# A two-block transformer forward pass on one core: later modulation, another router front end, expert sums on GpSimd, another order

## The chip, the cores and the metric

The kernel runs on 1 core of a Trainium2 chip. The metric is the time of one execution in device microseconds (us). A core has five engines that run their own instruction queues: TensorE (PE, matrix products and transposes), VectorE (DVE), ScalarE (ACT), GpSimd (POOL) and SyncE (SP, which here only issues transfers). Sixteen DMA engines move data between HBM and the on-chip memory (SBUF). Results of PE land in PSUM banks, from which DVE or ACT take them. An engine executes its queue in order: a waiting instruction holds everything behind it.

## The reference, cut to what matters

256 tokens of width 1024, all in fp32. Block 1 is one layer: retention and sliding-window attention side by side, then a mixture of experts (top 1 of 4 groups, top 2 of its 8 experts), then a gate fed by a second input `p`. Block 2 is two layers on the result `x` and on a context stream `ctx`, each layer with three branches and a feed-forward part, shifted and scaled by a modulation vector.

```python
# block 1
z = rms_norm(x, mix_norm_g) @ w_in
x = x + (sigmoid(gate_r) * retention(...) + sigmoid(gate_s) * attention(q, k, v)) @ w_out
h = rms_norm(x, ffn_norm_g)
g_prob = softmax(h @ w_rg + b_rg)               # 4 groups: the best one
e_logits = h @ w_re + b_re                      # its 8 experts: the best two
x = x + sum_over_two(weight * expert(h))        # SwiGLU, 1024 -> 256 -> 1024
x = x + sigmoid(rms_norm(x, ple_gate_norm_g) @ w_ple_gate) * rms_norm(p @ w_ple, ple_norm_g)
# block 2, twice
mod = silu(c) @ w_mod[l] + b_mod[l]             # 6 vectors of 1024; a second row for ctx
h = rms_norm_2(x, g_norm1) * (1 + sc1) + sh1
x = x + gt1 * (merge of 3 branches of h @ w_in[l]) @ w_out[l]
x = x + gt2 * relu(modulated norm(x) @ w1)**2 @ w2
```

The context stream goes through layer 0 in full; layer 1 takes only its keys and values.

## The kernel before, in words

Every dense weight arrives in pieces of 128x1024 fp32 (512 KB). SP loads a piece into `raw` (8 buffers, line L229), ACT rounds it into a high part `wh` (L187), DVE subtracts that from it to get the low part `wl` (L188), and PE makes three products for each (high·high, high·low, low·high): lines L245 to L247 where the weight is the stationary operand (`dense_a`), L268 to L270 where it moves (`dense_b`). So each piece costs a transfer, one ACT and one DVE pass, and 24 or 12 matmuls.

The program is one thread of Python that emits instructions; a tile scheduler then orders each engine's queue from dependences and priorities. Side jobs are generators put `beside` the main one: `advance()` moves each forward by a share of a step for each dense piece, `drain` runs the rest. Side jobs are: the modulation product `w_mod` of layer 0 during block 1 and that of layer 1 later (each step loads two pieces of `w_mod` at L704 and lets PE do four narrow matmuls with `sT` at L709), and the experts during the context's layer.

The stages: block 1's projections, first q, k, v of the windowed attention (L268 to L270 into `pd`), then its heads (transposes L533, L539, scores L551), retention, `w_out`. Then `router`: it loads its tables on the GpSimd queue (L736 to L746), sums squares of the rows of `xres` on ACT (L291), takes 1/rms by Newton steps on DVE (L178 to L183), scales the rows on DVE (L760), stores them to `xnscr` in HBM (L762), transposes them on PE (L767), multiplies by the router's weights (L772), and by a long chain of small steps forms the list of slots (PE L869, DVE L872). GpSimd gathers the rows of the first group of four experts into `m_he` (L913), PE transposes these (L925) and runs the experts: up and gate L935, down L954; weights lie in 8 buffers `ew`. Each group's result goes to `oscr` in HBM (L961). After the last group, GpSimd gathers each token's two results back into `m_ob` (L965, two buffers) and DVE adds weight times result to `xres` (L967). Then `moe_overflow` reads a count on every engine (L973) and branches over a rarely needed path (L974), and `ple_turn` normalizes `xres` (ACT L291, L322; DVE L321) and transposes it (L332) for the gate. The context stream's feed-forward part runs beside all that; its result `xc` is stored by GpSimd (L1654). After that come the two layers of x.

Of the kernel before, what the change touches and what calls it, by code (L numbers as in the profile page):

```python
# [9 lines left out]
F32 = mybir.dt.float32  # L10
# [10 lines left out]
D = 1024  # L21
T = 256
# [141 lines left out]
class Build:  # L164
    def __init__(self, nc, tc, ins, out, dbg=None):
# [5 lines left out]
        self.sturn = 0  # L171

# [66 lines left out]
    def mm_a(self, ps, x, w, f):  # L239
# [4 lines left out]
        for k, (wh, wl) in enumerate(w):  # L244
            mm(ps, wh[:, s], xh[:, k], start=k == 0, stop=False)  # L245
            mm(ps, wh[:, s], xl[:, k], start=False, stop=False)  # L246
            mm(ps, wl[:, s], xh[:, k], start=False, stop=k == n - 1)  # L247
# [9 lines left out]
    def dense_b(self, st, x, view, put, width=512):  # L257
# [3 lines left out]
        for c in range(0, view.shape[2], width):  # L261
            ps = [st.dense()[:, :width] for _ in range(2)]
            for k0, w in self.pieces(st, view[:, :, c:c + width]):
                for t in range(2):
                    s = slice(t * 128, t * 128 + 128)
                    for j, (wh, wl) in enumerate(w):
# [3 lines left out]
                        mm(ps[t], xl[:, k, s], wh, start=False, stop=k == K - 1)  # L270
# [86 lines left out]
    def run_all(self):  # L357
        nc, tc, i = self.nc, self.tc, self.i
        with ExitStack() as ctx:
# [114 lines left out]
    def block1_mix(self, st):  # L474
# [34 lines left out]
        self.dense_b(st, xT, w[:, :, 2560:2816], put_kv, width=256)  # L509
        gq8 = one.tile([128, 1], F32, name="gq8")  # L510
# [6 lines left out]
        nc.sync.dma_start(decay, i["decay"])  # L517
        rq = self.newton(st, ssq, 16, 1.0 / 64)
# [24 lines left out]
        for t in range(2):  # L543
# [32 lines left out]
            for hp in range(4):  # L576
# [8 lines left out]
                self.split(ysT[0][:, hp, ts], ysT[1][:, hp, ts], ps)  # L585

# [7 lines left out]
        STs = [held()[:, :768].rearrange("p (h s) -> p h s", h=2) for _ in range(2)]  # L594
# [99 lines left out]

    def w_mod(self, st, tag, l):
        nc, i = self.nc, self.i
        mm = nc.tensor.matmul
        for j in range(3):
            ps = self.psum.tile([128, 512], F32, name=tag, tag=tag, bufs=2)
            for k in range(8):  # L700
# [4 lines left out]
                with self.tc.high_priority(offset=CLUSTER):  # L705
                    for u in (1, 0):
                        for v in range(2):
                            g = 2 * u + v
                            mm(ps[32 * g:32 * g + 32], self.sT[:, k], wt[u][:, v * 512:v * 512 + 512], start=k == 0,  # L709
                               stop=False, tile_position=(0, 32 * g))  # L710
                yield
            brow = [self.weight(0) for _ in range(2)]
            for u in range(2):
                c = j * 2048 + u * 1024
                nc.sync.dma_start(brow[u][0:1], i["b_mod_2"][l:l + 1, c:c + 1024])
# [972 lines left out]
```

## Time and profile before

| | us |
|---|---|
| median of 3 runs (lowest, highest) | 1927.93 (1917.87, 1933.73) |
| the profiled execution, its own time | 1929.36 |
| its span in the trace | 1926.9 |
| PE busy in it | 1795.2 (93%) |
| DVE, ACT, GpSimd busy | 1245.0, 906.9, 215.4 |
| bytes moved, mean rate | 448.82 MB, 233 GB/s |

PE is the busiest engine in all stages. Its busy time isn't a constant: matmuls take about twice as long in stretches with half the granted clock, which the views of a stretch show as a granted clock under 1.00. So a stage is read by PE's idle time, by the granted clock, and by what ended the longest idle stretches.

### The profile page before, as it was taken

To read this page: it belongs to the slowest core of one execution; us is meant where nothing else is said; L and a number is where in the kernel's file an instruction comes from. 1 tells how busy PE (TensorE), PEld (TensorE's weight loads), DVE (VectorE), ACT (ScalarE), POOL (GpSimd) and SP (SyncE) were. 2 spreads that over 40 slices of the span, in tenths; PEclk is the share of its full clock that TensorE was granted. 3 is DMA by queue.
4 is the path that set the end of the run, shared out by engine and by line. 5 is a ranking of instruction groups with operands and counts; after the bars stand their busy time and mean duration, and the time that the engine had idled before them with its cause. 6 is when DMAs were issued, how large, how long until landed. Compare 5 with 4: busy or idle time off the path is not lost. (4 is left out here: it accounts for less than half of the span.)

```text
span 1926.9 us, 32425 instructions
## 1 busy us (share of the span) xinstructions
PE 1795.2 (93%) x12572; PEld 1474.3 (77%) x12572; DVE 1245.0 (65%) x2377; ACT 906.9 (47%) x1395; POOL 215.4 (11%) x209
## 2 busy tenths in 40 slices
PE   5999877999999999979899989999999899998998
PEld 3677856677786777765676878799998888787998
DVE  3554566664566545454768597866678887866665
ACT  3433434473444433334534465544456555554443
POOL 3000110100110101110121010011100210010110
PEclk9999988999999999989999999999999999998999
DMA  9788856889999998977787752555667655254652
GB/s 283 240 314 281 270 158 223 283 292 335 346 330 373 312 356 320 350 271 265 239 252 211 225 192 88 175 165 187 196 186 235 182 133 164 77 197 132 196 190 95
DMA packets 277172, 448.82 MB, mean 233 GB/s; under 512 B 35582, under 2 KB 182380, under 8 KB 276568
## 3 DMA queue, kind: packets, MB, share of 16 engines
q1 hardware_dynamic: 266344, 417.30, 65.0%
q0 software_dynamic: 10672, 29.43, 5.2%
q8 instruction: 99, 1.62, 0.3%
q14 instruction: 57, 0.47, 0.1%
HBM read 430.77 MB, written 15.86 MB: 232 GB/s over the span
## 5 line engine op out<-in xcount | busy, mean ns | idle before, releaser
L188 DVE TENSOR_TENSOR wl<-raw,wh 128x1024 fp32r<-128x1024 f32 (+2 forms) x484 | 610.3, 1265 | 366.5 <-ACT wh L187 207.3
L187 ACT ACTIVATE wh<-raw 128x1024 fp32r<-128x1024 f32 (+2 forms) x484 | 504.6, 1045 | 571.9 <-PE pd L246 117.6
L247 PE MATMUL pd<-xT,wl 128*128 128x256 f32 x384 | 108.9, 283 | 5.6 <-DVE wl L188 5.6
L245 PE MATMUL pd<-xT,wh 128*128 128x256 f32 x384 | 108.5, 283 | 0.4 <-DVE b_a L279 0.4
L246 PE MATMUL pd<-xT,wh 128*128 128x256 f32 x384 | 108.9, 283 | 0.0
L245 PE MATMUL cd<-b_a,wh 128*128 128x256 f32 x328 | 92.2, 281 | 0.0
L246 PE MATMUL cd<-b_a,wh 128*128 128x256 f32 x328 | 92.1, 281 | 0.0
L247 PE MATMUL cd<-b_a,wl 128*128 128x256 f32 x328 | 91.6, 279 | 0.0
L935 PE MATMUL ps<-ew,m_heT 128*32 128x256 f32 x1024 | 76.3, 386 | 8.2 <-DMA ew<-in_w_exp_up_dram 6.8
L247 PE MATMUL pd<-e_a,wl 128*128 128x256 f32 x288 | 82.3, 286 | 0.4 <-DVE wl L188 0.4
L245 PE MATMUL pd<-e_a,wh 128*128 128x256 f32 x288 | 82.4, 286 | 0.0
L246 PE MATMUL pd<-e_a,wh 128*128 128x256 f32 x288 | 81.8, 284 | 0.0
L246 PE MATMUL cd<-xT,wh 128*128 128x256 f32 x288 | 81.6, 283 | 0.0
L247 PE MATMUL cd<-xT,wl 128*128 128x256 f32 x288 | 81.3, 282 | 0.1
L245 PE MATMUL cd<-xT,wh 128*128 128x256 f32 x288 | 81.3, 282 | 0.0
L247 PEld LDWEIGHTS pd<-xT,wl 128*128 128x128 f32 x384 | 72.4, 189 | 8.8 <-DVE wl L188 6.4
L245 PEld LDWEIGHTS pd<-xT,wh 128*128 128x128 f32 x384 | 72.2, 188 | 4.3 <-issue 3.1
L246 PEld LDWEIGHTS pd<-xT,wh 128*128 128x128 f32 x384 | 72.2, 188 | 2.8 <-issue 2.5
L268 PE MATMUL cd<-wh,xT 128*128 128x512 f32 (+2 forms) x208 | 73.0, 352 | 0.0
L269 PE MATMUL cd<-wl,xT 128*128 128x512 f32 (+2 forms) x208 | 72.4, 348 | 0.1
L270 PE MATMUL cd<-wh,xT 128*128 128x512 f32 (+2 forms) x208 | 72.3, 348 | 0.0
L1609 POOL TENSOR_TENSOR xres<-xres,b_a 128x512 f32<-128x512 f32 x24 | 37.5, 1561 | 307.0 <-DVE b_a L1607 307.0
(719 smaller groups left out, 5036.7 us busy)
## 6 DMA issues: line engine op xcount, KB each, us to landing
raw<-in_ffn_w_dram SPq DMA_DIRECT2D x192, 512.0 KB, 4.6
raw<-in_w_in_dram SPq DMA_DIRECT2D x168, 512.0 KB, 5.2
raw<-in_w_mod_dram SPq DMA_DIRECT2D x96, 512.0 KB, 5.7
ew<-in_w_exp_gate_dram SPq DMA_DIRECT2D x64, 512.0 KB, 7.5
ew<-in_w_exp_up_dram SPq DMA_DIRECT2D x64, 512.0 KB, 8.3
ew<-in_w_exp_down_dram SPq DMA_DIRECT2D x64, 512.0 KB, 7.2
raw<-in_w_out_dram SPq DMA_DIRECT2D x32, 512.0 KB, 5.8
raw<-in_w_in_dram SPq DMA_DIRECT2D x16, 504.0 KB, 3.6
```

The source lines that it names most:

```text
L187: self.nc.scalar.activation(h, src, AF.Copy)
L188: self.nc.vector.tensor_tensor(l, src, h.bitcast(F32), op=ALU.subtract)
L245: mm(ps, wh[:, s], xh[:, k], start=k == 0, stop=False)
L246: mm(ps, wh[:, s], xl[:, k], start=False, stop=False)
L247: mm(ps, wl[:, s], xh[:, k], start=False, stop=k == n - 1)
L268: mm(ps[t], xh[:, k, s], wh, start=k == 0, stop=False)
L269: mm(ps[t], xh[:, k, s], wl, start=False, stop=False)
L270: mm(ps[t], xl[:, k, s], wh, start=False, stop=k == K - 1)
L935: mm(pg[32 * e:32 * e + 32, u * 256:u * 256 + 256], heT[:, kh * 4 + k, 32 * e:32 * e + 32], ws[e][:, k], start=kh == 0 and k == 0, stop=kh ...
L1609: (nc.vector if stats else nc.gpsimd).tensor_tensor(xs, xs, tmp, op=ALU.add)
```

## The change

Six edits. (1) The modulation of layer 0 starts after the q, k, v projections and not before them; the attention's head pairs advance it too; each step's matmuls are emitted one step late and are ordered behind the latest dense piece (`behind`, `strips`). (2) The router multiplies the transposed rows of `xres` as they are; the norm's gain is folded into the router's weights (`router_consts`, a GpSimd product over 128x288), the tables are loaded early on GpSimd's queue, and 1/rms is applied to the logits. Sums of squares are gathered as `w_out`'s results arrive. The scaled rows for `xnscr` are made by ACT and then by GpSimd (two products over 128x1024). (3) Two held buffers are taken earlier, and the second fetch of expert weights is emitted after the context layer's start. (4) The count is loaded as the last instruction before the branch on each engine. (5) The weighted sum of the expert results goes from one DVE instruction a gather to two on GpSimd: a product by the weight and an addition, each over 128x1024. (6) The tile scheduler orders with its timeline model.

```diff
-                mod = self.beside(self.w_mod(early, "cs", 0), MOD_EVERY)
                 mh = self.block1_mix(early)
+                mod = self.mod
...
-                for _ in range(2):
-                    self.fetch()
+                self.fetch()
                 cl.start()
+                self.fetch()
...
         self.dense_b(st, xT, w[:, :, 2560:2816], put_kv, width=256)
+        self.mod = self.beside(self.w_mod(st, "cs", 0), MOD_EVERY)
...
+        STs = [held()[:, :768].rearrange("p (h s) -> p h s", h=2) for _ in range(2)]
+        self.router_consts(held())
...
                 self.split(ysT[0][:, hp, ts], ysT[1][:, hp, ts], ps)
+                self.advance()
...
             nc.vector.tensor_tensor(xs, ps, xs, op=ALU.add)
+            self.stat(st, self.x, t, c)
...
+    def behind(self):
+        if self.last is not None and any(z is self.last for z in self.nc.cur_bb.bb.instructions):
+            return self.tc.issue_after(self.last)
+        return nullcontext()
+
+    def strips(self, ps, x, wt, start, stop):
+        with self.behind(), self.tc.high_priority(offset=CLUSTER):
+            for u in (1, 0):
+                for v in range(2):
+                    g = 2 * u + v
+                    self.nc.tensor.matmul(ps[32 * g:32 * g + 32], x, wt[u][:, v * 512:v * 512 + 512], start=start, stop=stop,
+                                          tile_position=(0, 32 * g))
...
+        nc.gpsimd.dma_start(wr[:, :, 0:4], kp(i["w_router_group"][0], 8))
+        nc.gpsimd.dma_start(wr[:, :, 4:36], kp(i["w_router_expert"][0], 8))
...
+        nc.gpsimd.tensor_tensor(wr, wr, gf[:, :, None].to_broadcast([128, 8, 36]), op=ALU.mult)
...
-        r = self.newton(st, self.sumsq(st, self.x), 2, 1.0 / D)
...
-                    nc.tensor.transpose(ps[:, kk, t * 128:t * 128 + 128], xn[:, t, 2 * j + kk], self.ident)
+                    nc.tensor.transpose(ps[:, kk, t * 128:t * 128 + 128], self.x[:, t, c:c + 128], self.ident)
...
+        r = self.inv_rms(st)
+        xn = act.a(8).rearrange("p (t k q) -> p t k q", t=2, k=8)
+        for t in range(2):
+            nc.scalar.activation(xn[:, t], self.x[:, t].rearrange("p (q k) -> p k q", k=8), AF.Copy, scale=r[t])
+            nc.gpsimd.tensor_tensor(xn[:, t], xn[:, t], gb.rearrange("p (q k) -> p k q", k=8), op=ALU.mult)
+            nc.gpsimd.dma_start(self.xnscr[t * 128:t * 128 + 128], xn[:, t].rearrange("p k q -> p (k q)"))
...
-                nc.vector.scalar_tensor_tensor(self.x[:, t], o, wk[:, t, k:k + 1], self.x[:, t], op0=ALU.mult, op1=ALU.add)
+                nc.gpsimd.tensor_scalar(o, o, wk[:, t, k:k + 1], None, op0=ALU.mult)
+                nc.gpsimd.tensor_tensor(self.x[:, t], self.x[:, t], o, op=ALU.add)
...
-        cnt = nc.values_load(self.flag[0:1, 0:1], min_val=0, max_val=T)
+        with ExitStack() as ctx:
+            seen = set()
+            for z in reversed(list(nc.cur_bb.bb.instructions)):
+                if z.engine not in seen and len(seen) < 5:
+                    seen.add(z.engine)
+                    ctx.enter_context(tc.issue_after(z))
+            cnt = nc.values_load(self.flag[0:1, 0:1], min_val=0, max_val=T)
...
-    with tile.TileContext(nc) as tc:
+    with tile.TileContext(nc, schedule_with_timeline_sim=True) as tc:
```

What that does to the queues is seen at three places. The first is SP's queue in the first stage. Before, pieces of block 1's `w_in` and of `w_mod` alternate:

```order
L229 DMA raw<-in_w_in_dram 128x2x512
L704 DMA raw<-in_w_mod_dram 128x1024 x2
L229 DMA raw<-in_w_in_dram 128x2x512
L704 DMA raw<-in_w_mod_dram 128x1024 x2
L229 DMA raw<-in_w_in_dram 128x4x256 x2
L515 DMA ew<-in_alibi_dram 128x1024 x2
L517 DMA ew<-in_decay_dram 128x1024
L704 DMA raw<-in_w_mod_dram 128x1024 x2
L229 DMA raw<-in_w_in_dram 128x4x256
```

And the same queue now, from the first `w_in` piece on:

```order
L230 DMA raw<-in_w_in_dram 128x2x512 x4
L230 DMA raw<-in_w_in_dram 128x4x256 x2
L519 DMA ew<-in_alibi_dram 128x1024 x2
L521 DMA ew<-in_decay_dram 128x1024
L724 DMA raw<-in_w_mod_dram 128x1024 x3
L353 DMA gc_ple_gate_norm_g<-in_ple_gate_norm_g_dram 128x8
L724 DMA raw<-in_w_mod_dram 128x1024 x11
L230 DMA raw<-in_w_in_dram 128x4x256
```

The six pieces of the q, k, v projections (the first two rows now) come first; 14 pieces of `w_mod` follow before the next `w_in` piece.

The second place is PE between the last slot matmul and the first transposes of gathered rows (`m_he`). Before, 72 matmuls stand between them, the two of row L1404 last; the start and the end of that piece:

```order
L869 MATMUL ps<-tok,slotS 128x1
L270 MATMUL cd<-wh,xT 128x336
L268 MATMUL cd<-wh,xT 128x336
L269 MATMUL cd<-wl,xT 128x336
...
L270 MATMUL cd<-wh,xT 128x256
L1404 MATMUL cs<-ident,c_ck 128x128 x2
L925 MATMUL ps<-ident,m_he 128x128 x7
```

And now, the whole piece:

```order
L890 MATMUL ps<-tok,slotS 128x1
L1432 MATMUL cs<-ident,c_ck 128x128 x2
L270 MATMUL cd<-wh,c_a_3011 128x512
L271 MATMUL cd<-wl,c_a_3011 128x512
L270 MATMUL cd<-wh,c_a_3011 128x512
L271 MATMUL cd<-wl,c_a_3011 128x512
L272 MATMUL cd<-wh,c_a_3012 128x512 x2
L270 MATMUL cd<-wh,c_a_3011 128x512
L271 MATMUL cd<-wl,c_a_3011 128x512
L272 MATMUL cd<-wh,c_a_3012 128x512
L946 MATMUL ps<-ident,m_he 128x128 x8
```

Between the slots and the gathered rows stand 11 matmuls now; the dense ones that were there have moved ahead of the slots.

The third place is the end of the experts. GpSimd's queue before, from the last store of an expert result to the store of `xc` (`ints` is the count; the rows left out are those of the branch):

```order
L961 DMA oscr<-m_ob 128x1024
L965 DMA m_ob<-oscr,ints 128x1024 x4
L973 TENSOR_LOAD ints
L974 COMPARE_AND_BRANCH
...
L974 UNCONDITIONAL_BRANCH
L1654 DMA ctxscr<-xc 128x2048
```

And now:

```order
L982 DMA oscr<-m_ob 128x1024
L986 DMA m_ob<-oscr,ints 128x1024 x2
L988 TENSOR_SCALAR m_ob<-m_ob,wk 128x1024 x2
L989 TENSOR_TENSOR xres<-xres,m_ob 128x1024 x2
L986 DMA m_ob<-oscr,ints 128x1024 x2
L1682 DMA ctxscr<-xc 128x2048
L988 TENSOR_SCALAR m_ob<-m_ob,wk 128x1024 x2
L989 TENSOR_TENSOR xres<-xres,m_ob 128x1024 x2
L1001 TENSOR_LOAD ints
L1002 COMPARE_AND_BRANCH
```

The sums stand on GpSimd, and the second pair of them stands behind the store of `xc`. PE's queue at the same branch, before (the context's matmuls stand on both sides of it; those behind it are 121 instructions up to the gate's transposes L332):

```order
L246 MATMUL cs<-c_a_6270,wh 128x256
L247 MATMUL cs<-c_a_6269,wl 128x256
L245 MATMUL cs<-c_a_6269,wh 128x256
L973 TENSOR_LOAD ints
L974 COMPARE_AND_BRANCH
...
L974 UNCONDITIONAL_BRANCH
L246 MATMUL cs<-c_a_6270,wh 128x256
L247 MATMUL cs<-c_a_6269,wl 128x256
L245 MATMUL cs<-c_a_6269,wh 128x256
```

And now:

```order
L270 MATMUL cs<-wh,c_a_8087 128x512
L271 MATMUL cs<-wl,c_a_8087 128x512
L272 MATMUL cs<-wh,c_a_8088 128x512
L1001 TENSOR_LOAD ints
L1002 COMPARE_AND_BRANCH
...
L1002 UNCONDITIONAL_BRANCH
L335 MATMUL ps<-ident,ew 128x128 x8
L270 MATMUL cd<-wh,ew 128x512
```

The rest of the context's feed-forward part, 139 matmuls after the last expert product, now stands ahead of the branch, and the gate's transposes L335 come first behind it.

## Rows read from the trace of the kernel before

**Rows 1.** The page: busy time of each engine over the span.

```profile
PE 1795.2 (93%) x12572; PEld 1474.3 (77%) x12572; DVE 1245.0 (65%) x2377; ACT 906.9 (47%) x1395; POOL 215.4 (11%) x209
```

**Rows 2.** Busy time by stretch: stretch, length, busy by engine, granted clock, DMA share, GB/s.

```profile
0.00:50.70 50.70, 29.97 (x146) 20.94 (x147) 19.06 (x49) 17.83 (x27) 18.29 (x31) 0.93 0.91 289
50.70:91.40 40.70, 38.09 (x278) 26.93 (x277) 25.43 (x91) 21.74 (x58) 4.48 (x7) 0.92 0.73 240
...
269.20:283.30 14.10, 4.99 (x15) 2.72 (x16) 7.46 (x17) 4.40 (x8) 1.07 (x2) 0.64 0.34 123
...
830.20:843.10 12.90, 5.91 (x28) 5.89 (x28) 5.96 (x6) 1.58 (x2) 3.87 (x4) 0.61 0.72 255
```

**Rows 3.** What PE waited for, 0 to 100 us: total, times, longest.

```profile
PE ps L332 <- DVE gq L511: 11.7, 1, 11.7
PE pd L268 <- ACT wh L187: 7.3, 3, 5.1
```

**Rows 4.** Timeline of ACT and PE in the first stage: start, duration, instruction, idle before.

```profile
40.44 1.06 ACT L187 ACTIVATE wh<-raw 128x1024 fp32r<-128x1024 f32 x1 [4.04 <-DMA raw<-in_w_in_dram]
...
51.55 1.06 PE L709 MATMUL cs<-raw,sT 128*32 128x512 f32 x8
```

**Rows 5.** Timeline of PE at 155 to 160 us.

```profile
158.74 1.93 PE L709 MATMUL cs<-raw,sT 128*32 128x512 f32 x8 [3.85 <-DMA raw<-in_w_mod_dram]
```

**Rows 6.** What PE waited for, 255 to 335 us (the router).

```profile
PE ps L767 <- issue: 7.8, 1, 7.8
...
PE ps L925 <- DMA m_he<-xnscr,ints: 3.8, 1, 3.8
```

**Rows 7.** Timeline of several engines in the router.

```profile
271.40 1.04 ACT L291 ACTIVATE r_junk<-xres 128x1024 bf16<-128x1024 f32 x1
...
274.74 4.03 DVE L760 SCALAR_TENSOR_TENSOR c_a<-xres,r_ny,c_a 128x1024 f32<-128x1024 f32 x2
...
302.92 0.16 DVE L872 CAST ints<-ps 128x8 int32<-128x8 f32 x1
...
315.69 1.72 PE L925 MATMUL ps<-ident,m_he 128*128 128x128 f32 x7 [3.80 <-DMA m_he<-xnscr,ints]
```

**Rows 8.** What PE waited for, 815 to 900 us (the end of the experts).

```profile
PE cd L247 <- DVE wl L188: 7.0, 1, 7.0
```

**Rows 9.** Timeline of several engines at the end of the experts.

```profile
819.73 1.04 PE L954 MATMUL pd<-ew,m_hidT 128*32 128x512 f32 x8
...
834.74 1.28 DVE L967 SCALAR_TENSOR_TENSOR xres<-m_ob,wk,xres 128x1024 f32<-128x1024 f32 x1 [9.61 <-DMA m_ob<-oscr,ints]
...
836.29 1.68 POOL L965 DMA_INDIRECT m_ob<-oscr,ints  x1 [4.73 <-DVE xres L967]
...
843.87 1.28 DVE L967 SCALAR_TENSOR_TENSOR xres<-m_ob,wk,xres 128x1024 f32<-128x1024 f32 x1 [3.18 <-DMA m_ob<-oscr,ints]
...
850.99 0.40 PE L270 MATMUL cd<-wh,c_a 128*128 128x512 f32 x1
851.23 0.40 PE L268 MATMUL cd<-wh,c_a 128*128 128x512 f32 x1
...
875.64 2.33 ACT L322 ACTIVATE ew<-xres,c_ny 128x1024 f32<-128x1024 f32 x1 [2.27 <-DVE c_ny L183]
...
880.76 1.04 PE L332 MATMUL ps<-ident,ew 128*128 128x128 f32 x8
```

**Rows 10.** Timeline of DVE and GpSimd in the last layer.

```profile
1782.42 2.37 POOL L1609 TENSOR_TENSOR xres<-xres,b_a 128x512 f32<-128x512 f32 x1 [1.83 <-DVE b_a L1607]
...
1787.89 1.23 DVE L188 TENSOR_TENSOR wl<-raw,wh 128x1024 fp32r<-128x1024 f32 x1 [1.52 <-PE ps L269]
...
1790.21 1.29 POOL L1609 TENSOR_TENSOR xres<-xres,b_a 128x512 f32<-128x512 f32 x1 [5.43 <-DVE b_a L1607]
1790.64 1.95 DVE L188 TENSOR_TENSOR wl<-raw,wh 128x1024 fp32r<-128x1024 f32 x1 [0.51 <-PE ps L269]
```

**Rows 11.** Groups of DVE instructions by line and shape: busy us, mean ns.

```profile
L321 DVE TENSOR_SCALAR ew<-xres,c_ny 128x1024 f32<-128x1024 f32 x1 | 1.3, 1304 | 0.0
```

More of the change, by code (lines that the diff above doesn't have):

```diff
@@ L1 @@
-from contextlib import ExitStack
+from contextlib import ExitStack, nullcontext
 import numpy as np
@@ L171, in __init__ @@
         self.sturn = 0
+        self.last = None
     def newton(self, st, ss, n, scale, eps=EPS, eng=None):
@@ L246, in mm_a @@
             mm(ps, wh[:, s], xl[:, k], start=False, stop=False)
-            mm(ps, wl[:, s], xh[:, k], start=False, stop=k == n - 1)
+            last = mm(ps, wl[:, s], xh[:, k], start=False, stop=k == n - 1)
+        self.last = last.ins
     def dense_a(self, st, x, view, put):
@@ L269, in dense_b @@
                         mm(ps[t], xh[:, k, s], wl, start=False, stop=False)
-                        mm(ps[t], xl[:, k, s], wh, start=False, stop=k == K - 1)
+                        last = mm(ps[t], xl[:, k, s], wh, start=False, stop=k == K - 1)
+                self.last = last.ins
             for t in range(2):
@@ L593, in block1_mix @@
         self.dense_b(st, xT, w[:, :, 1024:1536], lambda t, c, ps: self.evac(rv[:, t], ps))
-        STs = [held()[:, :768].rearrange("p (h s) -> p h s", h=2) for _ in range(2)]
         ST = [STs[h // 2][:, h % 2] for h in range(4)]
@@ L693, in mod_input @@
         nc.vector.memset(self.one, 1.0)
+    def behind(self):
[9 more added lines that the diff above has]
+                                          tile_position=(0, 32 * g))
     def w_mod(self, st, tag, l):
         nc, i = self.nc, self.i
-        mm = nc.tensor.matmul
         for j in range(3):
             ps = self.psum.tile([128, 512], F32, name=tag, tag=tag, bufs=2)
+            held = None
             for k in range(8):
@@ L704, in w_mod @@
                     nc.sync.dma_start(wt[u], pk(i["w_mod_2"][l], 8)[:, k, c:c + 1024])
[L705 to L710, printed above, removed]
+                if held:
+                    self.strips(*held)
+                held = (ps, self.sT[:, k], wt, k == 0, False)
                 yield
-            brow = [self.weight(0) for _ in range(2)]
+            brow = [self.weight(0)[0:1] for _ in range(2)]
             for u in range(2):
                 c = j * 2048 + u * 1024
-                nc.sync.dma_start(brow[u][0:1], i["b_mod_2"][l:l + 1, c:c + 1024])
-            with self.tc.high_priority(offset=CLUSTER):
-                for u in (1, 0):
-                    for v in range(2):
-                        g = 2 * u + v
-                        mm(ps[32 * g:32 * g + 32], self.one, brow[u][0:1, v * 512:v * 512 + 512], start=False, stop=True,
-                           tile_position=(0, 32 * g))
+                nc.sync.dma_start(brow[u], i["b_mod_2"][l:l + 1, c:c + 1024])
+            self.strips(*held)
+            self.strips(ps, self.one, brow, False, True)
             ev = (st or self.mst).a(2)
@@ L753, in router @@
         nc.gpsimd.dma_start(self.oscr[DUMP].rearrange("(p k) -> p k", k=8), zero)
-        r = self.newton(st, self.sumsq(st, self.x), 2, 1.0 / D)
         lgT = one.tile([36, 256], F32, name="lgT")
         lps = st.dense()
-        xn = act.a(8).rearrange("p (t k q) -> p t k q", t=2, k=8)
-        for t in range(2):
-            nc.vector.scalar_tensor_tensor(xn[:, t], self.x[:, t].rearrange("p (q k) -> p k q", k=8), r[:, t:t + 1],
-                                           gb.rearrange("p (q k) -> p k q", k=8), op0=ALU.mult, op1=ALU.mult)
-            nc.gpsimd.dma_start(self.xnscr[t * 128:t * 128 + 128], xn[:, t].rearrange("p k q -> p (k q)"))
         for j in range(4):
@@ L777, in router @@
             nc.tensor.transpose(ps[:, t * 36:t * 36 + 36], lgT[:, t * 128:t * 128 + 128], self.ident[:36, :36])
-        nc.vector.tensor_tensor(lg, ps[:, :72].rearrange("p (t e) -> p t e", t=2),
-                                br[:, None, :].to_broadcast([128, 2, 36]), op=ALU.add)
+        for t in range(2):
+            nc.vector.scalar_tensor_tensor(lg[:, t], ps[:, t * 36:t * 36 + 36], r[t], br, op0=ALU.mult, op1=ALU.add)
         tl = lambda shape, nm, dt=F32: one.tile(shape, dt, name=nm)
```

24 lines of the change are left out of this document (14 added, 10 removed).

## The prediction, made before the run

> **What bounds the kernel now.** I read the busy times first: PE is busy for 1795.2 of 1926.9 us and DVE, next, for 1245.0 [rows 1]. So PE bounds the whole, and only two things can change the time: PE's idle time, 131.7 us in all, and the stretches in which matmuls run at half clock. Then I read the stretches around the edits [rows 2] and what ended the idle time in each [rows 3, 6, 8], and last the timelines, which say what had held the releaser. Four places matter:
>
> In the first 50.7 us PE is busy for 29.97, so idle for 20.7. Of that, 11.7 is the wait for the first input and 7.3 is three waits for `wh` [rows 3]; ACT, which makes it, had waited for a piece of `w_in` to land [rows 4]. The mean granted clock is 0.93 [rows 2]: 0.07 x 50.7 = 3.5 us more.
>
> At 155 us PE waits 3.85 us for a piece of `w_mod`, and the eight narrow matmuls behind the wait take 1.93 us where they take 1.06 at full clock [rows 4, 5].
>
> In the router PE waits 7.8 us for the scaled rows and then 3.8 us for the gathered ones [rows 6]. In the 14.1 us around the first wait the granted clock is 0.64: half speed (1.2 for 2.4 GHz) right after the idle time, some 0.36 x 14.1 = 5.1 us [rows 2].
>
> At the end of the experts PE waits 7.0 us for one `wl` [rows 8], because DVE's queue stood for 9.61 us at the first weighted sum, whose gather hadn't landed [rows 9]. The clock there is 0.61 over 12.9 us, 5.0 us more [rows 2].
>
> **The change part by part**, against the profiled execution's own 1929.36 us, which is 1.4 above the median of three.
>
> Head. SP now asks for the six pieces of q, k, v first. The 7.3 us of waits should go, and the 3.5 us of slow clock with most of them: 10.8. Against that, 14 pieces of `w_mod` stand ahead of the next `w_in` piece: 14 x 0.524 MB at 289 GB/s [rows 2] is 25 us in which no new dense piece can come. The attention that follows is a chain of small steps, and PE is idle in it for only 2.6 of 40.7 us [rows 2], because dense matmuls and `w_mod` fill it. By the order of the changed kernel 60 dense matmuls stand in it for 108. Dense matmuls of 512 columns start 0.23 us apart [rows 9], those of 256 half of that, so 48 x 0.12 = 5.6 us of cover are gone. The deferred work isn't lost: it is done later. I take +8; the ends are -6 (waits stay in another form, and the cover lost is bare) and +13.4 (the 10.8 and the 2.6).
>
> Wait at 155 us. With strips a step late and the loads further ahead, it should go: +4; ends 0 and +7 (its slow clock too, by the 0.87 us that one group of eight lost, times the four or so in that stretch).
>
> Router. Transposes of the unscaled rows wait only for `w_out`'s sums, so the 7.8 us go. From the last sum of squares to the scaling took 3.3 us and the scaling 4.03 [rows 7]; both leave PE's path. But what ends the stage is the gather, and the slots lead to it: from the slots' cast at 302.92 to the transposes of gathered rows at 315.69 is 12.8 us [rows 7]. Before, 72 matmuls lay in it, and PE still waited 3.8. Now 11 lie there, 9 dense ones of 0.23 = 2 us, so PE should wait about 10 us at that point: the wait moves more than it goes. Idle time 7.8 + 3.8 before, about 10 after; with one slow stretch in place of two I take +3. The added GpSimd products (two over 128x1024, 2.6 us each, below), two stores and eight early table loads lie beside the slot chain; on GpSimd's early queue nothing urgent stands behind the tables. Without that cover the gather starts later by the two products: -5 is the low end. The high end is +13: 7.8 and 5.1 of clock, with the gathered rows no later than PE gets to them.
>
> The count. It is read late on every engine: its wait then comes after all work of the block, so it adds none of its own; before, it didn't delay anything that a row shows. 0.
>
> End of the experts. Let E be the last expert product's end, 820.8 [rows 9]. The first gather landed at 834.74, E + 14. A GpSimd addition over 128x512 takes 1.29 us when nothing disturbs it [rows 10], so 2.6 over 128x1024; no row shows a one-input product on GpSimd: DVE takes 1.30 for that shape [rows 11], and the two-input price of 2.6 is the other end. I take 1.3, since it reads half as much. Two products and two additions are 7.8 us: E + 22. Only then come the third and fourth gathers, which take 7.6 us from issue to use (836.29 to 843.87 [rows 9]): E + 30. Ahead of the second pair stands the store of `xc`, and `xc` needs the 139 context matmuls behind E (96 of 0.23 us and 43 of half that: 27 us) and some 3 us of sums: E + 30 as well. The second pair ends at E + 38. Then the sums of squares and Newton (3.3 us [rows 7]) and the scaling (2.33 [rows 9]): E + 44. PE is out of work at E + 27 and its next instructions are the gate's transposes, so it idles for 17 us. Before, the context's matmuls filled that time up to 880.76 [rows 9], at the price of the 7.0 us wait, which goes, since DVE no longer holds the gathers' wait. The slow clock after the new idle stretch costs about what the old one did. Net -10; the ends are -23 (second rival) and -4 (the store isn't late, and the pair is some us shorter).
>
> The rest of the program keeps its work, and only its order changes. Some 85 us of PE's idle time lie outside of these places, in waits of 1 to 6 us each; I see no sign by which the new order would lose or gain there, and put it at 0, with 10 either way.
>
> Sum: 8 + 4 + 3 - 10 = 5 faster, 1924.4 for the profiled execution, 1.4 less against the median: **1923 us**.
>
> **The rivals.** *The idle time goes and doesn't come back* (faster). Head 13, the wait at 155 us 7, router 13, end of the experts -4: 29 faster, 1899. For it: all four waits are queue-order waits, not a lack of bandwidth (the DMA share in the router is 0.34 [rows 2]). It decides at the slots: if the small DVE steps run earlier by 8 us or more, because DVE no longer scales rows, the gathered rows are there when PE comes.
>
> *The sums and the splits hold each other* (slower). A split that began inside a GpSimd addition took 1.95 us where its neighbour took 1.23, and a GpSimd addition beside a split took 2.37 where another took 1.29 [rows 10]. If all four additions meet splits they take 2.37/1.29 x 2.6 = 4.8 us, and the products 2.6: a pair is 14.7 us. The first ends at E + 29, the next gathers land at E + 37, the second pair ends at E + 51, the transposes start at E + 57: 30 us idle, 13 more than above, 1936. Against it: behind E + 27 there are few splits left to meet. It decides from the point where the first pair ends after `xc` is done. The Trainium skill's page "SBUF — State Buffer", section "Who interferes with whom", has this as a rule: GpSimd and a DVE instruction with two SBUF inputs take one pair of ports in turn, for a whole instruction. By that rule nothing is gained for DVE by the move, since it stands still while GpSimd adds; the trace agrees, with 1.95 for 1.23 us. The page "GPSIMD Engine Reference", section "Engine selection", puts two-input operations at about twice DVE's time and one-input ones near its rate; with that the sum stays as it is.
>
> *The attention runs bare* (slower). If the 25 us of `w_mod` transfers starve the attention, the head gives -6 and not +8: 1937. For it: a DMA share of 0.91 in that stretch already [rows 2]. With the second rival too: 1950.
>
> *The change doesn't do what it says*: the timeline order undoes the moved modulation or the early tables, and waits only change names: 1928.
>
> **How the numbers follow.** Chances: forecast (1911 to 1940 by the 10 either way) 0.38; first rival 0.31; second 0.12; third 0.08; both 0.08; the last 0.03. About 1% (19 us) is what a measurement of this kernel can tell from no change; three runs differ by 16 us. Faster by over 1% (below 1908.6) holds the first rival less its upper part, and a tail of the forecast: 0.36. Slower (above 1947.2): both rivals together, parts of each alone with a bad order elsewhere: 0.21. The rest, 0.43, is within 1%. The range is 1885 (first rival and a better order elsewhere) to 1951.
>
> **What would show it.** Right: PE's first long wait stays near 11.7 us and no wait for `wh` over 2 us follows; no wait at 155 us for `w_mod`; the router's transposes have no wait, and `m_he` one near 10 us; no 7 us wait for `wl` at the experts' end, but some 17 us at the gate's transposes, released by the chain behind GpSimd's second pair. The prediction is wrong if that last wait is under 5 us, if `m_he` is on time, or if PE's idle time behind 900 us changes by over 10 us.

## The result: slower, and the profile after

The changed kernel took 2008.22 us (median of 4 runs, 2004.36 to 2012.42) and the kernel before 1930.38 us beside it: a ratio of 1.041, 95% interval 1.038 to 1.045. So it is 78 us slower. The profiled execution took 2004.36 us, with a span of 2002.4.

The page's row of busy times answers to [rows 1]:

```profile
PE 1833.7 (92%) x12572; PEld 1492.4 (75%) x12572; DVE 1243.2 (62%) x2385; ACT 902.5 (45%) x1397; POOL 253.9 (13%) x221
```

The same 12572 PE instructions, and PE is busy for 38.5 us more. That is half of the loss, and my sum had no term in which PE's work could grow. The other half is idle time: span less busy time is 168.7 us where it was 131.7.

To find where PE's work grew I compared its groups of instructions by line and shape. First the two groups of expert matmuls before (gate and up, then down; each matmul leaves two records, so 1024 are 512 matmuls; then busy us, mean ns, and idle time just ahead of them):

```profile
L935 PE MATMUL ps<-ew,m_heT 128*32 128x256 f32 x1024 | 76.3, 386 | 8.2 <-DMA ew<-in_w_exp_up_dram 6.8 <-DMA ew<-in_w_exp_gate_dram 1.1 <-ACT m_heT L277 0.2
L954 PE MATMUL pd<-ew,m_hidT 128*32 128x512 f32 x256 | 38.0, 600 | 0.7 <-DVE m_hidT L948 0.5
```

And after:

```profile
L956 PE MATMUL ps<-ew,m_heT 128*32 128x256 f32 x1024 | 96.8, 395 | 11.7 <-DMA ew<-in_w_exp_gate_dram 6.1 <-DMA ew<-in_w_exp_up_dram 5.2
L975 PE MATMUL pd<-ew,m_hidT 128*32 128x512 f32 x256 | 57.1, 599 | 0.0
```

The mean of one is the same, 386 and 395 ns, 600 and 599, while the union of their times went from 114.3 to 153.9 us: 39.6 more. So one matmul is no slower; fewer of them overlap. An expert matmul is a strip: it uses 32 of the 128 columns, and the code emits four of them, one for each expert of the group, for four different sets of columns. In the timeline of PE in the changed kernel the runs of strips are cut by other matmuls:

```profile
345.75 0.64 PE L1472 MATMUL cs<-ident,c_a 128*96 128x128 f32 x4
346.23 0.38 PE L1432 MATMUL cs<-ident,c_a 128*128 128x128 f32 x2
346.54 0.63 PE L956 MATMUL ps<-ew,m_heT 128*32 128x256 f32 x4
347.19 0.44 PE L1432 MATMUL cs<-ident,c_a 128*128 128x128 f32 x2
347.56 0.62 PE L956 MATMUL ps<-ew,m_heT 128*32 128x256 f32 x2
...
349.35 1.91 PE L956 MATMUL ps<-ew,m_heT 128*32 128x256 f32 x26
```

One strip by itself takes 0.62 us, two take 0.63, and 13 take 1.91 (x2 is one matmul, x26 are 13). A group cut in two is paid twice. Counted in PE's queue, the 512 gate and up strips (128 groups of four) are cut into 153 pieces of groups before and 184 after: 31 more at 0.62 us would be 19 of the 20.5 us by which these strips grew.

The down strips grew by 19.1 us, and not only by cuts: the new order also puts strips of one expert next to each other, which use the same 32 columns. Before, PE's queue has no such neighbours; in the changed kernel it has 15 pairs, and twelve runs consist of one such pair alone. The last of them is the first PE row of the timeline further down: two strips in 1.90 us, where four on different columns took 1.04 [rows 9]. Twelve such runs at 0.86 us more are some 10 of the 19.1 us, by this estimate; the rest wasn't taken apart.

The idle time: what PE waited for in the first 100 us answers to [rows 3]:

```profile
PE cs L712 <- DMA raw<-in_w_mod_dram: 17.6, 6, 5.1
PE ps L335 <- DVE e_a L324: 13.0, 1, 13.0
PE pd L246 <- ACT wh L188: 3.5, 1, 3.5
```

The 7.3 us of waits for `wh` in the q, k, v projections are gone, as forecast, and 17.6 us of waits for `w_mod` came in their place. By stretch, against the first two of [rows 2] (the cut is the first transpose of the attention in both):

```profile
0.00:41.30 41.30, 24.83 (x129) 18.64 (x129) 22.78 (x65) 18.44 (x29) 27.24 (x44) 0.98 0.92 267
41.30:96.70 55.40, 35.10 (x204) 23.38 (x200) 17.62 (x68) 15.80 (x49) 6.54 (x10) 0.77 0.79 221
```

The attention starts 9.3 us earlier and lasts 55.4 us where it lasted some 38; in it PE is idle for 20.3 us instead of 2.6, and the granted clock is 0.77 instead of 0.92.

The router answers to [rows 6]: the 7.8 us are gone. The longest waits there that don't concern expert weights:

```profile
PE cs L1432 <- DVE c_ck L1427: 2.9, 1, 2.9
PE ps L946 <- DMA m_he<-xnscr,ints: 2.6, 1, 2.6
```

Both lie between the last slot matmul and the gathered rows, with two shorter ones of 1.0 and 0.5 us, so PE is idle there for 7.0 us in all. The end of the experts answers to [rows 8 and 9]. What PE waited for, 860 to 980 us, and the timelines of GpSimd, PE, ACT and DVE there:

```profile
PE ps L335 <- DVE ew L324: 20.8, 1, 20.8
PE ps L335 <- issue: 11.4, 1, 11.4
```

```profile
882.95 1.90 PE L975 MATMUL pd<-ew,m_hidT 128*32 128x512 f32 x4
...
896.31 2.85 POOL L988 TENSOR_SCALAR m_ob<-m_ob,wk 128x1024 f32<-128x1024 f32 x1 [3.06 <-DMA m_ob<-oscr,ints]
900.46 3.04 POOL L988 TENSOR_SCALAR m_ob<-m_ob,wk 128x1024 f32<-128x1024 f32 x1 [1.30 <-DMA m_ob<-oscr,ints]
903.47 6.46 POOL L989 TENSOR_TENSOR xres<-xres,m_ob 128x1024 f32<-128x1024 f32 x2
...
914.85 0.59 POOL L1682 DMA_DIRECT2D ctxscr<-xc  x1 [1.68 <-DVE xc L1637]
915.94 2.85 POOL L988 TENSOR_SCALAR m_ob<-m_ob,wk 128x1024 f32<-128x1024 f32 x1 [0.50 <-DMA m_ob<-oscr,ints]
920.63 2.85 POOL L988 TENSOR_SCALAR m_ob<-m_ob,wk 128x1024 f32<-128x1024 f32 x1 [1.84 <-DMA m_ob<-oscr,ints]
923.45 4.75 POOL L989 TENSOR_TENSOR xres<-xres,m_ob 128x1024 f32<-128x1024 f32 x2
...
928.23 1.06 ACT L294 ACTIVATE c_junk<-xres 128x1024 bf16<-128x1024 f32 x1 [11.25 <-POOL xres L989]
...
905.08 7.07 DVE L189 TENSOR_TENSOR wl<-raw,wh 128x1024 fp32r<-128x1024 f32 x3 [0.77 <-ACT wh L188]
```

With E = 884.9 the first pair of sums ends at E + 25 and the second at E + 43; the transposes start at 932.9, E + 48. That is the chain that I forecast, with an idle time of 20.8 us for 17. The second row of waits, 11.4 us, stands ahead of the first transpose of x in layer 0; before, that wait was

```profile
PE ps L332 <- issue: 6.5, 1, 6.5
```

It is 9.9 us with the first edit alone and 6.6 with the router alone (runs below), so it comes with the first edit; by what path was not tried. The whole stretch from E to that transpose, before and after:

```profile
820.80:924.50 103.70, 83.77 (x417) 58.54 (x417) 59.36 (x109) 46.79 (x66) 5.91 (x6) 0.94 0.75 258
884.90:975.90 91.00, 58.31 (x283) 44.09 (x284) 50.18 (x97) 38.57 (x56) 29.07 (x14) 0.84 0.60 201
```

PE is idle there for 32.7 us and not 19.9. The stretch is still 12.7 us shorter, since PE has 25.5 us less work in it: matmuls of the context moved ahead of E.

The two layers of x lost too. Busy times by stretch, from the turn of x in layer 0 to that of layer 1, and on to the last feed-forward part, before:

```profile
924.50:1245.00 320.50, 307.49 (x2150) 249.91 (x2151) 240.45 (x541) 166.72 (x281) 40.18 (x34) 0.99 0.64 199
1245.00:1738.50 493.50, 468.43 (x3237) 418.87 (x3235) 371.65 (x714) 265.74 (x415) 52.34 (x36) 0.99 0.57 171
```

And after, in stretches that end at the same places of the program:

```profile
975.90:1309.50 333.60, 313.08 (x2183) 254.26 (x2184) 241.93 (x542) 164.86 (x283) 40.72 (x34) 0.97 0.66 200
1309.50:1812.50 503.00, 474.56 (x3237) 424.95 (x3235) 370.94 (x715) 263.87 (x413) 55.70 (x36) 0.97 0.56 168
```

They are 13.1 and 9.5 us longer: 7.5 and 3.4 us of idle time, and 5.6 and 6.1 us of PE's busy time at a clock of 0.97 for 0.99; the first holds 33 more records of PE. So the profiled span grew by 10.6 us up to the first gathered rows, by 53.5 in the experts, by 22.6 in these two stretches and by 1.5 behind them, less the 12.7.

### The profile page after: what moved, and what is told of

Its sections match the earlier page's. It is cut to its first block, busy times and chain, and to the rows that moved or that the text cites. A ratio compares the mean times of both kernels' runs of the same rounds, so it can differ in the third digit from the quotient of the medians.

```text
span 2002.4 us, 32466 instructions
## 1 busy us (share of the span) xinstructions
PE 1833.7 (92%) x12572; PEld 1492.4 (75%) x12572; DVE 1243.2 (62%) x2385; ACT 902.5 (45%) x1397; POOL 253.9 (13%) x221
## 4 chain that ended last, share of the span: by engine, by line
PE 72%; DMA 10%; DVE 9%; issue 4%; ACT 3%; POOL 1%; SPq 1%; POOLq 0%; ACTq 0%; DVEq 0%
PE cd L246 5%; DMA raw<-in_w_in_dram 5%; PE cd L248 4%; PE cd L247 4%; PE pd L248 4%; PE cd L270 4%; PE pd L246 4%; PE cd L271 4%; PE pd L247 4%; PE cd L272 4%; PE ps L956 3%; DVE wl L189 3%; PE pd L270 3%; PE pd L271 3%; PE pd L272 3%
## 5 line engine op out<-in xcount | busy, mean ns | idle before, releaser
L956 PE MATMUL ps<-ew,m_heT 128*32 128x256 f32 x1024 | 96.8, 395 | 11.7 <-DMA ew<-in_w_exp_gate_dram 6.1
L1637 POOL TENSOR_TENSOR xres<-xres,b_a 128x512 f32<-128x512 f32 x24 | 43.0, 1800 | 300.2 <-DVE b_a L1635 300.2
L956 PEld LDWEIGHTS ps<-ew,m_heT 128*32 128x32 f32 x1024 | 35.4, 112 | 52.0 <-issue 14.4
L270 PE MATMUL cd<-wh,xT 128*128 128x512 f32 (+2 forms) x208 | 72.3, 352 | 1.7 <-ACT c_a L1585 1.7
```

The costliest lines, as they stand in the source:

```text
L270: mm(ps[t], xh[:, k, s], wh, start=k == 0, stop=False)
L956: mm(pg[32 * e:32 * e + 32, u * 256:u * 256 + 256], heT[:, kh * 4 + k, 32 * e:32 * e + 32], ws[e][:, k], start=kh == 0 and k == 0, stop=kh ...
L1637: (nc.vector if stats else nc.gpsimd).tensor_tensor(xs, xs, tmp, op=ALU.add)
```

## The experiments

Theory 1: the timeline order is what costs, most of it by cutting the groups of strips. Theory 2: the other five edits cost. Theory 3: cut groups only fill time in which PE would have waited for weights. All ratios are to the kernel before, measured beside each run. A difference between two kernels is taken from their ratios; 1% is 19 us, and each such difference is good to about 7 us. The expectations put the gate and up strips at 83 us before and 104 after, and the down strips at 38 and 54; the profile lines above have 76.3 and 96.8, 38.0 and 57.1, and those are used here.

### The order and the edits apart

The changed kernel in the default order, and the kernel before in the timeline order:

```diff
-    with tile.TileContext(nc, schedule_with_timeline_sim=True) as tc:
+    with tile.TileContext(nc) as tc:
```

> The changed kernel with the scheduler's default order, the other five edits kept. Theory 1 (the timeline order is what costs; most of it by cutting the groups of four expert strips, which PE runs side by side, 184 pieces of groups for 153 before): the loss goes nearly whole, 1915 to 1945 us, and the gate/up strips take about 83 us as before and not 104. Theory 2 (the five edits cost: sums on GpSimd, later modulation): 1985 to 2010 us.

> The kernel before with the timeline order alone. Theory 1 (the order costs): 1975 to 2000 us, with the gate/up strips at about 100 us and the down strips at about 52. Theory 2 (the edits cost, the order is neutral): 1920 to 1945 us.

The first took 1932.66 us (ratio 1.004, 1.002 to 1.006), the second 1976.90 us (1.026, 1.023 to 1.030). The order alone costs 2.6%, 51 us; on top of the five edits it costs 3.7% (1.041 for 1.004), 71 us; the five edits in the default order cost 8 us. Theory 2 falls for all but these 8 us. The strips go with the order. Changed kernel, default order:

```profile
L956 PE MATMUL ps<-ew,m_heT 128*32 128x256 f32 x1024 | 75.3, 385 | 6.7 <-DMA ew<-in_w_exp_up_dram 5.8 <-DMA ew<-in_w_exp_gate_dram 0.6 <-ACT m_heT L280 0.3
```

Kernel before, timeline order:

```profile
L935 PE MATMUL ps<-ew,m_heT 128*32 128x256 f32 x1024 | 94.8, 397 | 13.1 <-DMA ew<-in_w_exp_up_dram 6.9 <-DMA ew<-in_w_exp_gate_dram 6.2
L954 PE MATMUL pd<-ew,m_hidT 128*32 128x512 f32 x256 | 51.4, 599 | 0.0
```

Together that is 31.9 us more than the 114.3 of the kernel before in its own order.

### Whole groups, first way: it priced something else

Each step's strips as one unit for the scheduler, in the changed kernel and in the kernel before (the down strips likewise):

```diff
-                    for k in range(4):
-                        for e in range(4):
-                            mm(pg[32 * e:32 * e + 32, u * 256:u * 256 + 256], ...)
+                    with self.tc.tile_critical():
+                        for k in range(4):
+                            for e in range(4):
+                                mm(pg[32 * e:32 * e + 32, u * 256:u * 256 + 256], ...)
```

> The changed kernel, timeline order kept, but the 16 gate/up strips of a step and the 8 down strips of a step each made one unit for the scheduler, so that no group of four is cut. Theory 1 (cut groups are about half of the loss): the strips fall from 104 and 54 us to about 62 and 31, less some 10 us since a unit waits for the last of its four weights: 1950 to 1970 us. Theory 3 (the order costs by its waits elsewhere, the cut groups only fill time that PE would have waited anyway): 1995 to 2010 us.

> The kernel before with the same units. Theory 1: its strips take 83 and 38 us for 62 and 31 when whole, so 15 to 28 us are to be had: 1900 to 1915 us. Theory 3: no gain, 1925 to 1940 us, as units wait for their last weight and PE idles instead.

They took 2223.57 us (1.153, 1.148 to 1.157) and 2073.55 us (1.076, 1.073 to 1.080). Every expectation missed, and the waits say why. What PE waited for in the first of them:

```profile
PE ps L957 <- DMA raw<-in_ffn_w_dram: 44.0, 10, 7.0
...
PE ps L957 <- DMA raw<-in_w_in_dram: 40.4, 5, 9.2
```

The gate and up strips (L957) wait for loads of dense weights that they don't read, as if such a unit began only when other work in flight has landed. These two runs price that barrier, not cut groups, and tell nothing between the theories.

### Whole groups, second way

The strip whose weight is loaded last comes first, and the others are queued behind it at a high priority. No barrier is added. The down strips are emitted likewise. In both, neighbours are strips of different experts, so the edit undoes the cuts and the pairs on the same columns at once:

```diff
+    def together(self, strips):
+        with self.tc.high_priority(offset=2000):
+            f, a, b = strips[0]
+            first = f(a, b)
+            with self.tc.issue_after(first):
+                for f, a, b in strips[1:]:
+                    f(a, b)
...
+                    self.together([(strip, k, e) for k in range(4) for e in (3, 2, 1, 0)])
```

> The changed kernel in the timeline order, with the last expert's strip first in each step and the others right behind it at a high priority: no group of four is cut (128 and 32 pieces for 184 and 46), and no engine gets a barrier. Theory 1 (cut groups cost PE time): the strips fall from 104 and 54 us to about 60 and 31; 1945 to 1970 us. Theory 3 (the pieces fill time that PE would wait for weights anyway): PE waits for weights by as much more, 1995 to 2010 us.

> The kernel before with the same edit, default order (128 and 32 pieces for 153 and 44). Theory 1: its strips fall from 83 and 38 us to about 60 and 31; 1895 to 1915 us. Theory 3: 1920 to 1935 us.

The changed kernel fell to 1959.53 us (1.014, 1.011 to 1.017): 2.7% or 52 us less. Its strips:

```profile
L963 PE MATMUL ps<-ew,m_heT 128*32 128x256 f32 x1024 | 67.3, 408 | 7.1 <-DMA ew<-in_w_exp_gate_dram 4.6 <-DMA ew<-in_w_exp_up_dram 2.5
L983 PE MATMUL pd<-ew,m_hidT 128*32 128x512 f32 x256 | 31.9, 620 | 2.4 <-DMA ew<-in_w_exp_down_dram 2.4
```

99.2 us for 153.9, so 54.7 less, and the time fell by as much within its uncertainty: theory 1 holds there. (The edit puts expert steps at other places in the queue too, so this isn't the groups alone.) The kernel before gained nothing, 1930.29 us (1.000, 0.997 to 1.004), though its strips fell by 16.3 us to 98.0. Its gate and up strips:

```profile
L942 PE MATMUL ps<-ew,m_heT 128*32 128x256 f32 x1024 | 68.3, 413 | 17.4 <-DMA ew<-in_w_exp_up_dram 11.6 <-DMA ew<-in_w_exp_gate_dram 4.8 <-DVE m_heT L279 0.8
```

The wait ahead of them rose from 8.2 to 17.4 us: here theory 3 holds. The stretch of the experts shows the limit: the kernel before, then the changed one:

```profile
315.70:820.80 505.10, 487.96 (x3824) 370.15 (x3824) 278.69 (x473) 215.13 (x332) 48.13 (x46) 0.98 0.91 327
```

```profile
326.30:884.90 558.60, 535.50 (x3917) 386.01 (x3918) 287.59 (x478) 217.35 (x333) 49.35 (x46) 0.98 0.85 304
```

Before, the DMA engines were busy for 0.91 of that stretch, and PE's work of 488 us just fitted beside them. After, PE's work there is 535.5 us, by the 39.6 more of the strips and by matmuls of the context that moved there (93 more records in all), and PE, not the transfers, set the length (DMA share 0.85). With whole groups in the changed kernel the share is back at 0.91:

```profile
328.40:840.00 511.60, 471.60 (x3798) 369.32 (x3799) 293.73 (x469) 210.21 (x324) 79.94 (x59) 0.96 0.91 331
```

By that reading making groups whole gives back what PE had over the transfers, and no more.

### What a group costs when its strips don't overlap

The kernel before with whole gate and up steps, but all four strips of one expert in a row; the down strips keep the order of the run above (the expectation wrongly counted them in):

```diff
-                    self.together([(strip, k, e) for k in range(4) for e in (3, 2, 1, 0)])
+                    self.together([(strip, k, e) for e in (3, 2, 1, 0) for k in range(4)])
```

> The kernel before with whole steps at high priority, but the strips of one expert in a row, so that neighbours write the same 32 rows. Theory 1 (four strips on four different row groups run side by side and cost what one costs): 512 gate/up strips of some 0.46 us and 128 down strips of 0.92 take 230 and 118 us for 68 and 29, and the time is 2080 to 2200 us. If strips cost the same in any order: 1922 to 1940 us, as with the other order of whole steps.

1985.24 us (1.032, 1.027 to 1.036), less than expected: the down strips didn't pay, and the gate and up strips take 149.4 us, not 230. The same 16 strips of a step in the timeline of PE, side by side (the run with whole groups in the kernel before), then in a row:

```profile
449.09 1.93 PE L942 MATMUL ps<-ew,m_heT 128*32 128x256 f32 x32
```

```profile
406.11 4.59 PE L942 MATMUL ps<-ew,m_heT 128*32 128x256 f32 x32
```

A factor of 2.4, without any other matmul between them; all gate and up strips take 149.4 us for 68.3. So neighbours on different columns overlap and those on the same columns hardly do, and what breaks the neighbourhood costs PE time. The time rose by 61 us (1.000 to 1.032) for these 81; some of the rest came out of the waits for weights, 7.9 us ahead of these strips for 17.4.

### The sums

Back on DVE, in the timeline order and in the default order:

```diff
-                nc.gpsimd.tensor_scalar(o, o, wk[:, t, k:k + 1], None, op0=ALU.mult)
-                nc.gpsimd.tensor_tensor(self.x[:, t], self.x[:, t], o, op=ALU.add)
+                nc.vector.scalar_tensor_tensor(self.x[:, t], o, wk[:, t, k:k + 1], self.x[:, t], op0=ALU.mult, op1=ALU.add)
```

> The changed kernel in the timeline order, with the weighted sums back on DVE. If the 20.8 us wait at the gate's transposes comes from the sums on GpSimd behind the store of xc, it falls under 10 us and the time to 1990 to 2000 us. If it comes from the order (no matmuls left behind the branch), the wait stays within 4 us of 20.8 and the time at 2003 to 2013 us.

> The changed kernel in the default order with the sums on DVE. If the sums on GpSimd are what the edits lose there (10.0 us wait at the gate's transposes, which the kernel before has not): 1920 to 1928 us. If the wait of 7 us for a split comes back in its place, as in the kernel before: 1930 to 1936 us.

In the timeline order 1993.27 us (1.032, 1.029 to 1.035), 0.9% or 18 us less than the changed kernel, and the wait at the gate's transposes fell from 20.8 to

```profile
PE ps L335 <- DVE ew L324: 6.5, 1, 6.5
```

So the sums behind the store of `xc` cost some 14 to 18 us there. In the default order 1940.92 us (1.006, 1.004 to 1.008), above both expectations and no better than with the sums on GpSimd (1.004): the wait of 10.0 us goes and one of 6.7 us for a split comes back. There the place of the sums is worth nothing either way.

### The first two edits

The first edit alone, the router alone, and edits 2 to 5 in both orders (the diffs are those pieces of the change):

> The kernel before with the first edit alone (modulation after the q, k, v projections, strips a step late), default order. The windowed attention should end some 11 us earlier, as in the run of all five edits in that order. Theory A (the DMA engines are the limit up to the router, so the moved w_mod pieces hold up the dense pieces behind the attention): PE waits 10 us or more for weights between the attention and the router, and the time is 1925 to 1940 us. Theory B (the head's gain stays): 1912 to 1920 us.

> The kernel before with the router edit alone, default order. By the prediction's term (the wait of 7.8 us goes, the wait for the gathered rows grows): 1922 to 1928 us. By the first rival (both waits go): 1910 to 1918 us. By a theory that the GpSimd products delay the gather: 1930 to 1938 us with a wait for the gathered rows over 8 us.

> Edits 2 to 5 without the later modulation, default order. Theory A: without the first edit what is lost ahead of the router comes back, 1915 to 1927 us. Theory B (the loss of the five edits lies in the router or the sums): 1930 to 1940 us.

> Edits 2 to 6, so the timeline order without the later modulation. If the later modulation makes the waits for w_mod at 36 to 66 us (17.6 us in the changed kernel): 1985 to 1998 us. If the timeline order makes them by itself, as the kernel before in that order suggests (14.3 and 6.7 us of waits for w_mod in other places): 2003 to 2013 us.

| kernel | median us | ratio (95%) |
|---|---|---|
| first edit alone | 1939.06 | 1.004 (1.002 to 1.006) |
| router alone | 1915.27 | 0.991 (0.988 to 0.994) |
| edits 2 to 5, default order | 1916.81 | 0.992 (0.988 to 0.996) |
| edits 2 to 6, timeline order | 1977.87 | 1.024 (1.020 to 1.028) |

The first edit alone loses 8 us. What PE waited for in that run between 60 and 260 us:

```profile
PE pd L246 <- ACT wh L188: 17.7, 4, 7.6
```

The attention's last transposes (of its weights, ahead of the product with v) end at 74 us there and at 88 in the kernel before; then the dense pieces wait for weights that stand behind `w_mod` pieces in SP's queue. The gain of the head is given back, as theory A of that run has it. Its reason, that the DMA engines are the limit, isn't shown: they are busy for 0.78 of the first 200 us there and for 0.85 in the kernel before. With edits 2 to 5 beside it the first edit costs 1.2%, 24 us, in the default order (1.004 for 0.992) and 1.8%, 34 us, in the timeline order (1.041 for 1.024); the run without it there came out under both expectations. In that order the 17.6 us of waits for `w_mod` at the head are gone without it, and 18.2 us of waits for `wh` stand in the projections instead. The order on top of edits 2 to 5 costs 3.2%, 61 us.

The router alone gains 0.9%, 17 us, as the first rival had it, and not 3. PE's wait for the gathered rows in that run is

```profile
PE ps L935 <- DMA m_he<-xnscr,ints: 2.8, 1, 2.8
```

and no wait for the transposes of `xres` is over 2 us. The whole chain moved: its slots are cast at 290.7 us where [rows 7] have 302.92. (The execution in this profile, 1924.59 us, is the slowest of five, so its places are read here and not its length.)

That gain doesn't show beside the first edit: the first edit alone and all five edits in the default order have the same ratio, 1.004. PE reaches the gathered rows at 303.7 us with the router alone, for 315.7 before, but at 328.0 with the first edit alone and at 331.7 with all five. In the timeline order edits 2 to 5 together change 1.026 to 1.024, which is within the uncertainty.

### The order without the rest, and the best of both

Edits 2 to 4 in the timeline order with whole groups, and the router alone in the default order with whole groups:

> The timeline order with edits 2 to 4 only (modulation early, sums on DVE) and the groups of four strips kept whole. Edits 2 to 6 in that order took 1978 us. Theory 1 (of the order's cost most is the cut groups, and the later modulation and the sums behind the store of xc make up the rest of the loss): 1918 to 1935 us. Theory 4 (the order loses over 20 us more in the two layers of x and in the head): 1940 to 1960 us.

> The router edit alone in the default order (1915 us) with the groups kept whole. If the weights' arrival limits the experts in that order, as for the kernel before with whole groups (1930 for 1929 us): 1908 to 1922 us. If the router's gain lets whole groups pay: 1890 to 1905 us.

1939.24 us (1.005, 1.002 to 1.009) and 1917.11 us (0.995, 0.993 to 0.997). The first, between its two expectations, lies 1.8% or 35 us under edits 2 to 6 in that order, and 22 us above the second, which is in the default order. The second lacks edits 3 and 4; in the default order edits 3 to 5 add nothing to the router (0.992 for 0.991). So with cut groups and the sums out of the way the order still loses some 20 us; in the two profiles PE reaches the experts 15 us later, and the two layers of x with all that follows take 13 us more, with 7 us given back in between. Which instructions lose it was not tried. Whole groups add nothing to the router edit in the default order, where the DMA share of the experts' stretch is 0.90.

The best versions are the router alone and edits 2 to 5 in the default order, 1915 and 1917 us: 0.8 to 0.9% under the kernel before and 5% under the changed one.

## Why the prediction was wrong, point by point

**The step that failed** is the last of the sum: "The rest of the program keeps its work, and only its order changes", at 0 with 10 us either way. The work of a strip isn't a constant. Four strips on different columns take about what one takes, so an order that puts other matmuls between them, or strips on the same columns next to each other, makes PE's work longer: 39.6 us more of it here, and 52 us of the time when undone. The cut runs could be read in the changed kernel's queue before the run, and one strip's price from the trace; I compared waits alone. The same term failed in the two layers of x as well, which lost 22.6 us, 10.9 of them idle time: by the prediction's own sign it was wrong there; why is open. My reading that only PE's idle time and its clock can change the time left this out from the start.

**Head**: the term was +8, the third rival -6. The projections did end 9.3 us earlier, and the wait for `w_mod` and the slow clock in the attention took more than that: up to the attention's last transposes the kernel is 8.5 us later (96.7 for 88.2), with some `w_mod` groups still to come. The third rival was right on the mechanism. What I put too low is what follows: the pieces of `w_mod` that left the head stand in front of the dense pieces behind it, and the first edit alone loses 8 us in the default order as well.

**Wait at 155 us**: gone, as forecast; no wait for `w_mod` is left there. It is small against what came at 36 to 66 us.

**Router**: the term was +3 with a wait of 10 us for the gathered rows; that wait is 2.6 us, and with the three in front of it 7.0. So the thin cover behind the slots was read rightly for the changed kernel, and the waits have other names than forecast. For the edit alone the first rival was right: 17 us. Beside the first edit that gain doesn't show.

**The clock's price** was too high. It was taken as the missing share of the clock times the length of the stretch, 5.1 and 5.0 us in the router and at the end of the experts. But PE is busy for only 4.99 and 5.91 us there [rows 2] (less than DVE, with 7.46 and 5.96, so PE isn't the busiest engine in every stretch), and at half clock matmuls take about twice as long (1.93 us for 1.06 [rows 4, 5]). So about half of PE's busy time, some 2.5 and 3 us, is the most that can be lost. The high end of the router and the head's 10.8 rest on the same reckoning.

**End of the experts**: the mechanism and the place were right, a new wait at the gate's transposes with the second pair of sums behind the store of `xc`. It was 17 us and measured 20.8. PE's idle time from E to layer 0 rose by 12.8 us, 4.9 of them in the wait ahead of layer 0, so the net of -10 came near. The size that was wrong is that of the one-input product: 2.85 to 3.04 us on GpSimd, not 1.3 and not near the 1.30 that DVE takes [rows 11]; it is above the other end of 2.6 as well. The second rival's mechanism shows in the first pair, whose two additions take 6.46 us for the 4.75 of the second pair, which met no splits. Sums on DVE give some 18 us back.

**The count**: no wait on it shows in the changed kernel, as forecast.

The parts don't add up to exactly 78 us, since each was measured beside others: the order 51 to 71 (whole groups alone give back 52 in the changed kernel, the sums 18, and about 20 stay open in place), the first edit 8 to 34 by what stands beside it, the router -17 alone, and edits 2 to 5 together nothing beside the first in the default order.

## What to carry to other kernels

When a scheduler's order changes, compare not only which instructions wait but which stand next to each other: in this kernel matmuls that run side by side on parts of the array are cheap only as neighbours on different parts, and a queue with the same instructions can hold more work. Take apart a change of order and changes of code, and the edits from each other: here an edit worth 17 us alone came to nothing beside another, and an order that cost 71 lay over both. And where transfers fill a stage to 0.9, as the experts' stage here, making PE's work shorter only changed the name of the wait.

## What was unexpected of the hardware

A GpSimd product of one tensor by a value for each partition is dearer than its two-tensor addition over the same 128x1024: 2.85 us for 2.38 (4.75 for two) with DVE quiet. Of the three splits in the row of 7.07 us the first two met GpSimd's first pair of additions, the third came after it:

```profile
905.08 2.58 DVE L189 TENSOR_TENSOR wl<-raw,wh 128x1024 fp32r<-128x1024 f32 x1 [0.77 <-ACT wh L188]
907.75 3.27 DVE L189 TENSOR_TENSOR wl<-raw,wh 128x1024 fp32r<-128x1024 f32 x1
910.94 1.21 DVE L189 TENSOR_TENSOR wl<-raw,wh 128x1024 fp32r<-128x1024 f32 x1
```

The two take 2.58 and 3.27 us for 1.21, and the additions beside them 3.10 and 3.28 for 2.33: each holds up the other. Two down strips on the same columns take 1.90 us where eight alternating ones take 1.92 (in the runs with whole groups). And a strip of 32 columns alone takes 0.62 us where 16 of them side by side take 1.93, 0.12 each.
